# First pages and squares re-dealt, and the compressed decode branch laid out in rows, in a hybrid-decoder step on one core

## The chip, the cores and the metric

One core of a Trainium2 chip runs the kernel. The metric is device time in microseconds of one execution, the median of three. A measurement of this kernel can tell some 0.2% (2.3 us) from no change.

## The reference

One layer of a decoder step for 256 prompt tokens and 8 decode requests with 2048 past tokens each. RMS-normed inputs (2048 wide) go through one wide projection `w_in` in fp32. Two token mixers follow: sparse attention in three branches (compressed, selected, window) and a gated DeltaNet. Their outputs are gated, projected (`w_pa`, `w_pb`), merged, projected once more (`w_o`) and added to the input. The part that the change touches is the compressed branch of the decode requests:

```python
def nsa_sample(q, kv_cmp, kv_slc, kv_win, cache_cmp, cache_slc, st_win, page_table, cw, slopes):
    past = cache_cmp[page_table].reshape(DB, past_len, 2, NSA_KV_HEADS, HEAD_DIM)
    pk_past, pv_past = compress_partials(past, cw)      # conv over 16-token strides with w1
    kc, vc = compress_finish(...)                       # silu, w2, rms_norm of keys: 127 compressed K, V rows
    o_cmp, p_cmp = cmp_attend(q, kc, vc, qpos, slopes)  # softmax(q kc * SCALE - slope * distance) vc
    idx, valid = select_blocks(p_cmp, qpos, kc.shape[1], ...)   # top 16 blocks by summed p_cmp
    o_slc = slc_sample(...)                             # attention over the selected blocks, gathered from the cache
    o_win, _ = dense_gqa(...)                           # attention over the last 512 tokens
```

There are 8 requests, 2 key/value groups and 4 query heads per group: 64 softmax rows of 127 compressed keys. Each branch's output is scaled by a sigmoid gate per head; the three are added.

## The kernel before

The program is one long loop over "halves" (lines 1623 to 1636). A half is a block of 1024 rows of weights (512 KB) times the normed input, or a quarter of one request's pages of the compressed cache times `w1`: 24 matmuls of 254 or 264 columns, since each fp32 operand is split into `hi` (ScalarE, ACT) and `lo` (VectorE, DVE), both fp32r, and three of the four products are made. Turn i of the loop issues the load of half i+4, the split of half i+2 and the matmuls of half i; `hi` and `lo` have three buffers each.

Between a half's two parts, and behind it, stands `tick()`. Everything else (the input norm, the finishing of compressed keys, decode branches, prompt attention, DeltaNet) is a generator that a tick takes on to its next `yield`; `yield n` skips to the n-th tick from there. Ticks begin at turn -1: turn i makes ticks 2i+3 and 2i+4. Turns 0, 2, 4 and 6 load `w1` and have no matmuls; turns 1, 3, 5, 7 and from 8 on are page halves, four to a request; after the 24th come the projections of `kvc`, the first that need the normed input. Four parts of x, of four 128-row blocks each, are marked as they are ready; the program runs ticks ahead of a projection until the part that it needs is marked.

DMA queues of SP and POOL (GpSimd) keep the program's order. On PE (TensorE), ACT and DVE the framework that builds the kernel takes, among the instructions that are ready by its estimate, the one that the program issued first; the order is then fixed.

Big tiles share one pool of 13 slots (`slot()`, tag `s8`): cache pages, the input, `q`, keys, gates, DeltaNet tiles, gathered keys and values (`gk`, `gv`), probabilities (`sP`, `wP`) and the branch outputs `X`. A tile holds its slot until its last access.

Start: `load_pages` issues request 0's 16 pages of 128 KB over SP, POOL and ACT in turn (line 384), each after a `value_load` of its page number. `g_xnorm` (line 279) loads the parameters (`prm`), later constants (`cst`), then the input (`xt`), squares it on ACT, reduces over blocks on DVE (line 295), sums over partitions on PE (`xss`), takes a reciprocal root in 12 DVE steps (`rsq`, line 212), scales `xt` (line 306) and splits it into `xh`, `xl`.

The decode branches run one after the other (`g_dec_cmp`, `g_dec_slc`, `g_dec_win`, then `g_oa`). `g_dec_cmp` puts the 127 keys on partitions: for each group and request it multiplies that request's keys (128 columns of weights) with all 64 queries (`dcs`) and keeps the 4 columns that belong (`diag`); likewise the values (`dcv`). The result, scaled by `gd`, goes to `oD`. The other two branches use a row layout: 128 softmax rows, 32 for each of four column groups of PE, of which 16 are in use; products there have 32 columns of weights (`qk`, `gsc`, `wsc`, `pvo`). Their outputs `X0` and `X1` are turned into columns by `smo`, one product for each request and branch, and added to `oD`. `g_gdn` (DeltaNet of the prompt) and the `z` projections wait for what `g_oa` copies from `oD`.

Of the kernel before, what the change touches and what calls it, by code (L numbers as in the profile page):

```python
# [55 lines left out]
def shape_constants():  # L56
# [19 lines left out]
    sl64 = np.broadcast_to(slope.reshape(2, 1, 4), (2, NB, 4)).reshape(64)  # L76
    c.add("cmpb", -(PAST - kendd)[:, None] * sl64[None])
# [67 lines left out]
def program(tc, A):  # L145
# [93 lines left out]
    gd = cp.tile([128, 64], F32, name="gd")  # L239
    grow = cp.tile([128, 2], F32, name="grow")  # L240
# [132 lines left out]
    rawc = {}  # L373

    def load_pages(kv, b, part):
# [7 lines left out]
        for j in range(4 * part, 4 * part + 4):  # L383
            e = (SP, G, S)[j % 3] if kv + b == 0 else (SP, G)[j % 2]
# [218 lines left out]
    def g_small(ps):  # L603
# [24 lines left out]
        mm(p2[:, 0:64], ones[0:24, :], x[:, 0:2].rearrange("p a b r -> p (a b r)"))  # L628
        S.activation(gd, p2[:, 0:64], AF.Copy)
        xp = tp.tile([24, 2, 2, 2, 32], F32, name="gxp", tag="a", bufs=NA)  # L630
        V.memset(xp, 0.0)
        for br in range(2):
            for c in range(2):
                V.tensor_copy(xp[:, br, c, :, 0:16].rearrange("p g (i r) -> p g i r", r=4),
                              x[:, 2 + 2 * br:4 + 2 * br].rearrange("p a (i c) r -> p c a i r", c=2)[:, c])
            mm(p2[:, 192 + br:193 + br], xp[:, br].rearrange("p c g x -> p (c g x)"), ones[0:24, 0:1])
        V.tensor_copy(grow, p2[:, 192:194])
# [3 lines left out]
    def diag(ps, dst, g):
        d = dst[:, 32 * g:32 * g + 32].rearrange("p (b r) -> p b r", r=4)
        return [(d[:, 0:7], ps[:, 0:476].rearrange("p (b c) -> p b c", c=68)[:, :, 32 * g:32 * g + 4], slice(0, 7)),
                (d[:, 7:8], ps[:, 476 + 32 * g:480 + 32 * g].unsqueeze(1), slice(7, 8))]


    def g_dec_cmp():
# [3 lines left out]
        SCm = tp.tile([128, 64], F32, name="dcs", tag="dcs")  # L651
        E = tp.tile([64, 128], F32, name="dce", tag="zz", bufs=2)
        PT = tp.tile([128, 64], F32, name="dcp", tag="dcp")
        m1 = tp.tile([64, 4], F32, name="dcm", tag="dcm")
        qf = qd.rearrange("p g b r -> p (g b r)")
# [9 lines left out]
        p2 = psb("dct")
        tr(p2[0:64, 0:127], SCm[0:127, :])
        V.tensor_reduce(m1[:, 0:1], p2[0:64, 0:127], AX.X, ALU.max, negate=True)
        S.activation(E[:, 0:127], p2[0:64, 0:127], AF.Exp, bias=m1[:, 0:1], accum_out=m1[:, 1:2])
        V.reciprocal(m1[:, 2:3], m1[:, 1:2])
        V.tensor_scalar(E[:, 0:127], E[:, 0:127], m1[:, 2:3], None, ALU.mult)  # L670
# [15 lines left out]
        mark("oD")  # L686
# [78 lines left out]
    def row_softmax(sc, n, w):  # L765
# [8 lines left out]
        V.tensor_mul(sn[:, 3:4], sn[:, 3:4], grow[:, w:w + 1])  # L774
# [33 lines left out]
    def pv_take(po, w, b):  # L808
        if b % 4 == 3:
            S.activation(L["X", w][:, b - 3:b + 1, :], po.rearrange("p (b d) -> p b d", b=4), AF.Copy)  # L810

    def g_dec_win():
# [40 lines left out]
        sc = bb[:, 1]  # L853
        yield 7
# [24 lines left out]
        del L["X", 0], L["X", 1]  # L879
        mark("oD")  # L880

    def g_dec_slc():
# [13 lines left out]
        GP, VP = 1, 1  # L896
# [37 lines left out]
        L["X", 0] = slot("X0", [128, NB, 128])  # L934
        yield 2
        for b in range(NB):
# [6 lines left out]
            pv_take(po, 0, b)  # L943
# [798 lines left out]
```

## Time and profile before

| | |
|---|---|
| time, three runs | 1136.26, 1136.46, 1137.62 us (median 1136.46) |
| profiled execution | 1137.88 us, its span 1136.2 us |
| PE busy | 1112.4 us (98%) |
| DVE, ACT, POOL busy | 697.1, 572.7, 144.2 us |
| DMA | 222.17 MB, mean 196 GB/s |
| mean granted clock of PE | 0.994 |

The span runs from the first to the last instruction; the metric is a little longer. Engines: PE is TensorE's matmul, PEld its weight load. A product of plain fp32 appears as two instructions. Times in the rows below are us from the span's start.

### The profile page before, as it was taken

To read this page: it belongs to the slowest core of one execution; us is meant where nothing else is said; L and a number is where in the kernel's file an instruction comes from. 1 tells how busy PE (TensorE), PEld (TensorE's weight loads), DVE (VectorE), ACT (ScalarE), POOL (GpSimd) and SP (SyncE) were. 2 spreads that over 40 slices of the span, in tenths; PEclk is the share of its full clock that TensorE was granted. 3 is DMA by queue.
4 is the path that set the end of the run, shared out by engine and by line. 5 is a ranking of instruction groups with operands and counts; after the bars stand their busy time and mean duration, and the time that the engine had idled before them with its cause. 6 is when DMAs were issued, how large, how long until landed. Compare 5 with 4: busy or idle time off the path is not lost.

```text
span 1136.2 us, 25323 instructions
## 1 busy us (share of the span) xinstructions
PE 1112.4 (98%) x9558; PEld 1069.3 (94%) x9558; DVE 697.1 (61%) x1523; ACT 572.7 (50%) x1138; POOL 144.2 (13%) x227
## 2 busy tenths in 40 slices
PE   4999999999999999999999999999999999999998
PEld 3989999999999987897989999999999999999998
DVE  3578565443657776783566577677547575487443
ACT  4445655444634766673454465545344554444332
POOL 4430244200001310113022100102000000000000
PEclk9989999999999999999999899999999999999999
DMA  9873676435445784568998755657454355556663
GB/s 302 255 241 124 202 205 203 152 95 160 161 138 177 218 214 135 159 196 220 281 390 291 268 174 176 201 179 220 138 187 148 119 165 177 181 184 223 201 236 125
DMA packets 77069, 222.17 MB, mean 196 GB/s; under 512 B 10625, under 2 KB 27850, under 8 KB 75410
## 3 DMA queue, kind: packets, MB, share of 16 engines
q1 hardware_dynamic: 59346, 164.36, 44.7%
q0 software_dynamic: 15008, 44.98, 13.8%
q10 hardware_dynamic: 2592, 11.21, 2.6%
q8 instruction: 75, 1.23, 0.4%
q14 instruction: 48, 0.39, 0.1%
HBM read 202.90 MB, written 17.60 MB: 194 GB/s over the span
## 4 chain that ended last, share of the span: by engine, by line
PE 92%; DVE 1%; ACT 0%; issue 0%; ACTq 0%
PE acc L205 77%; PE inv L205 1%; PE po L205 1%; PE gtr L202 1%; PE pvo L205 1%; PE ps L205 1%; PE gsc L205 1%; PE cf L205 1%; PE kk L205 1%; PE vnb L202 1%; PE uw L205 1%; DVE xt L306 1%; PE pst L202 0%; PE og L205 0%; PE wsc L205 0%; PE kvtr L202 0%
## 5 line engine op out<-in xcount | busy, mean ns | idle before, releaser
L333 DVE TENSOR_TENSOR lo<-raw,hi 128x1024 fp32r<-128x1024 f32 (+1 forms) x250 | 304.8, 1220 | 212.5 <-ACT hi L332 206.1
L205 PE MATMUL acc<-xh,hi 128*128 128x264 f32 (+1 forms) x1488 | 433.8, 292 | 0.0
L332 ACT ACTIVATE hi<-raw 128x1024 fp32r<-128x1024 f32 (+1 forms) x250 | 263.9, 1056 | 329.7 <-PE acc L205 269.0
L205 PE MATMUL acc<-xl,hi 128*128 128x264 f32 (+1 forms) x1488 | 426.9, 287 | 0.5 <-issue 0.5
L205 PE MATMUL acc<-xh,lo 128*128 128x264 f32 (+1 forms) x1488 | 426.3, 287 | 0.0
L205 PEld LDWEIGHTS acc<-xh,hi 128*128 128x128 f32 (+1 forms) x1488 | 281.0, 189 | 7.6 <-issue 7.0
L205 PEld LDWEIGHTS acc<-xh,lo 128*128 128x128 f32 (+1 forms) x1488 | 280.0, 188 | 2.7 <-issue 2.2
L205 PEld LDWEIGHTS acc<-xl,hi 128*128 128x128 f32 (+1 forms) x1488 | 281.1, 189 | 1.5 <-issue 1.0
L205 PE MATMUL acc<-hi,w1h 128*128 128x254 f32 (+1 forms) x512 | 148.1, 290 | 15.9 <-ACT hi L409 15.9
L205 PE MATMUL acc<-lo,w1h 128*128 128x254 f32 (+1 forms) x512 | 147.4, 288 | 3.4 <-DVE lo L410 3.2
L205 PE MATMUL acc<-hi,w1l 128*128 128x254 f32 (+1 forms) x512 | 145.7, 285 | 0.0
L410 DVE TENSOR_TENSOR lo<-rawc,hi 128x512 fp32r<-128x512 f32 (+2 forms) x136 | 84.0, 656 | 52.5 <-ACT hi L409 48.1
L205 PEld LDWEIGHTS acc<-hi,w1h 128*128 128x128 f32 x512 | 98.4, 192 | 16.0 <-ACT hi L409 15.9
L409 ACT ACTIVATE hi<-rawc 128x512 fp32r<-128x512 f32 (+2 forms) x136 | 74.7, 599 | 62.7 <-PE acc L205 58.0
L205 PEld LDWEIGHTS acc<-lo,w1h 128*128 128x128 f32 x512 | 99.2, 194 | 4.8 <-DVE lo L410 4.5
L205 PEld LDWEIGHTS acc<-hi,w1l 128*128 128x128 f32 x512 | 99.0, 193 | 0.1
L386 POOL DMA_DIRECT2D rawc<-ccmp x125 | 67.3, 538 | 98.2 <-issue 72.3
L205 PE MATMUL acc<-oh,hi 128*128 128x264 f32 x256 | 73.5, 287 | 0.0
L205 PE MATMUL acc<-oh,lo 128*128 128x264 f32 x256 | 72.9, 285 | 0.0
L205 PE MATMUL acc<-ol,hi 128*128 128x264 f32 x256 | 72.7, 284 | 0.0
L205 PE MATMUL acc<-mh,hi 128*128 128x264 f32 x256 | 72.6, 284 | 0.0
L205 PE MATMUL acc<-ml,hi 128*128 128x264 f32 x256 | 72.5, 283 | 0.0
(452 smaller groups left out, 1476.4 us busy)
## 6 DMA issues: line engine op xcount, KB each, us to landing
raw<-win SPq DMA_DIRECT2D x184, 512.0 KB, 3.5
raw<-wpab SPq DMA_DIRECT2D x32, 512.0 KB, 3.9
raw<-wo SPq DMA_DIRECT2D x32, 512.0 KB, 4.3
rawc<-ccmp SPq DMA_DIRECT2D x126, 128.0 KB, 2.7
rawc<-ccmp POOLq DMA_DIRECT2D x125, 128.0 KB, 3.3
raw<-w SPq DMA_DIRECT2D x8, 512.0 KB, 7.6
wk<-winK SPq DMA_DIRECT2D x8, 512.0 KB, 11.1
o_wk<-wk POOLq DMA_DIRECT2D x8, 512.0 KB, 9.0
```

The source lines that it names most:

```text
L202: T.transpose(out, in_, ident[0:n, 0:n])
L205: T.matmul(out, lhsT, rhs, start=start, stop=stop, **k)
L306: V.scalar_tensor_tensor(xt[i][:, k, :], xt[i][:, k, :], P("nw")[:, kk:kk + 1], rx, ALU.mult, ALU.mult)
L332: S.activation(self.hi, self.raw, AF.Copy)
L333: V.tensor_sub(self.lo, self.raw, self.hi)
L386: e.dma_start(rawc[kv, b][j // 8][:, j % 8].rearrange("p s c g -> p (s c g)"), src[kv, bass.ds(r, 1)].rearrange("o d f -> (o d) f"))
L409: S.activation(h, src, AF.Copy)
L410: V.tensor_sub(l, src, h)
```

## The change

1. Request 0's pages are dealt by a list `FIRST`: 7 to SP, 6 to ACT, 3 to POOL (6, 5, 5 before). `prm` is issued three ticks later, `cst` and `xt` one tick later.
2. The squares of x are made in halves of four blocks with a tick between; the reduction over 8 blocks becomes three adds of 4, 2 and 1 blocks. In ticks the sum over partitions moves from 43 to 50.
3. `g_dec_cmp` uses the row layout: scores by `qk` with 32-column weights, key norms spread over rows by a transpose and a product, softmax over 128 rows, values by 32 products of 64 (63) rows and 32 columns of weights, outputs into one `X`.
4. The other branches add into the same `X` (DVE, from PSUM) instead of having their own; `smo` has 8 products for `X` instead of 16. The gates of all three branches come in row form (`grow`, three columns; `gd` goes).
5. In `g_dec_win` the second value load is issued before the scores, the others one step earlier; in `g_dec_slc` value gathers run two requests ahead instead of one.

```diff
-    c.add("cmpb", -(PAST - kendd)[:, None] * sl64[None])
+    c.add("kd", np.broadcast_to(-(PAST - kendd)[None], (128, NCMP)))
...
     def g_xnorm():
+        yield 3
         G.dma_start(prm, A["prm"])
+        yield 5
         V.tensor_scalar(hb[:, 0:1], P("b1k"), 0.5, None, ALU.mult)
         V.tensor_scalar(hb[:, 1:2], P("b1v"), 0.5, None, ALU.mult)
-        yield 7
         G.dma_start(cst, A["cst"])
...
         for i in range(2):
-            S.activation(sq, xt[i], AF.Square)
-            V.tensor_reduce(a2[i], sq.rearrange("p k t -> p t k"), AX.X, ALU.add)
+            for k in range(2):
+                S.activation(sq[:, 4 * k:4 * k + 4], xt[i][:, 4 * k:4 * k + 4], AF.Square)
+                yield
+            V.tensor_add(sq[:, 0:4], sq[:, 0:4], sq[:, 4:8])
+            yield
+            V.tensor_add(sq[:, 0:2], sq[:, 0:2], sq[:, 2:4])
+            V.tensor_add(a2[i], sq[:, 0], sq[:, 1])
+            yield
         V.tensor_add(a2[0], a2[0], a2[1])
-        yield 5
+        yield 3
...
+    FIRST = (SP, S, G, SP, S, SP, S, G, SP, S, G, SP, S, SP, S, SP)
...
-            e = (SP, G, S)[j % 3] if kv + b == 0 else (SP, G)[j % 2]
+            e = FIRST[j] if kv + b == 0 else (SP, G)[j % 2]
...
     def g_dec_cmp():
...
-        for g in range(2):
-            pt = psb("dcs")
-            for b in range(NB):
-                mm(pt[0:127, 64 * b:64 * b + 64], L["kcT"][:, b, g, :], qf)
-            for o, pv, w in diag(pt[0:127], SCm[0:127], g):
...
-        V.tensor_add(SCm[0:127], SCm[0:127], C("cmpb", 127))
+        tr(p2[0:16, 0:127], rkc[0:127])
+        rkt = tp.tile([16, 128], F32, name="rkt", tag="imp")
+        V.tensor_copy(rkt[:, 0:127], p2[0:16, 0:127])
+        mm(p2[:, 128:255], C("e64", 16), rkt[:, 0:127])
+        S.activation(rkr, p2[:, 128:255], AF.Copy)
+        pt = psb("dcs")
+        for i in range(4):
+            qk(pt, i, lambda c, g: L["kcT"][:, 2 * i + c, g, :])
+        V.tensor_mul(SC, pt[:, 0:127], rkr)
+        V.scalar_tensor_tensor(SC, C("kd"), C("c64")[:, 1:2], SC, ALU.mult, ALU.add)
...
         yield 5
...
+        tr(p3[0:127, 0:128], SC)
...
+        V.tensor_scalar(SC, SC, grow[:, 0:1], None, ALU.mult)
         yield 3
-        for g in range(2):
-            p5 = psb("dcv")
-            for b in range(NB):
-                mm(p5[:, 64 * b:64 * b + 64], L["vc"][0:127, b, g, :], PT[0:127, :])
-            for (o, pv, _), (_, gv, _) in zip(diag(p5, oD, g), diag(p5, oD, g)):
-                V.tensor_copy(o, pv)
-        V.tensor_mul(oD, oD, gd)
+        tr(p3[0:127, 128:256], SC)
+        S.activation(PT[0:127], p3[0:127, 128:256], AF.Copy)
...
+        yield 2
+        L["X"] = slot("X", [128, NB, 128])
+        for b in range(NB):
+            if b % 4 == 0:
+                po = PV("pvo")
+            for g in range(2):
+                for t, rows in enumerate((slice(0, 64), slice(64, 127))):
+                    j, c, o = 2 * g + t, 2 * (b % 2) + g, 128 * (b % 4)
+                    mm(po[32 * j:32 * j + 32, o:o + 128], PT[rows, 32 * c:32 * c + 32], L["vc"][rows, b, g, :])
+            if b % 4 == 3:
+                S.activation(L["X"][:, b - 3:b + 1, :], po.rearrange("p (b d) -> p b d", b=4), AF.Copy)
...
-    def pv_take(po, w, b):
+    def pv_take(po, b):
         if b % 4 == 3:
-            S.activation(L["X", w][:, b - 3:b + 1, :], po.rearrange("p (b d) -> p b d", b=4), AF.Copy)
+            x = L["X"][:, b - 3:b + 1, :]
+            V.tensor_add(x, x, po.rearrange("p (b d) -> p b d", b=4))
...
+        load_v(1)
         yield 7
         scores([ps], sc, bb[:, 0])
...
-            if b % 2 == 0 and b < 6:
-                load_v(b // 2 + 1)
+            if b % 2 == 0 and b < 4:
+                load_v(b // 2 + 2)
...
-        for w in range(2):
-            for b in range(NB):
-                mm(o[:, :, b, :], L["X", w][:, b, :], gx[:, :, b, :], start=False, stop=w * b == 7)
-        V.tensor_add(oD, oD, pt[:, 0:64])
+        for b in range(NB):
+            mm(o[:, :, b, :], L["X"][:, b, :], gx[:, :, b, :], start=False, stop=b == 7)
+        V.tensor_copy(oD, pt[:, 0:64])
...
-        GP, VP = 1, 1
+        GP, VP = 1, 2
```

## Rows read from the trace of the kernel before

**Rows 1.** The page: the span, and PE's busy time with its share and instructions.

```profile
span 1136.2 us, 25323 instructions
...
PE 1112.4 (98%) x9558; PEld 1069.3 (94%) x9558; DVE 697.1 (61%) x1523; ACT 572.7 (50%) x1138; POOL 144.2 (13%) x227
```

**Rows 2.** PE's waits of the whole span: who waited for whom, then us in total, times, longest.

```profile
PE acc L205 <- ACT hi L409: 15.9, 1, 15.9
...
PE acc L205 <- DVE lo L410: 3.2, 2, 2.6
...
PE pvo L205 <- ACT wP L798: 0.6, 1, 0.6
```

**Rows 3.** Stretches of the first 100 us: from:to, length, then busy us and instructions of PE, PEld, DVE, ACT and POOL, granted clock of PE, share of the DMA engines, GB/s.

```profile
40.00:50.00 10.00, 10.00 (x85) 9.95 (x85) 5.37 (x10) 5.62 (x12) 4.07 (x9) 1.00 0.72 224
...
71.00:72.00 1.00, 0.00 (x0) 0.00 (x0) 1.00 (x3) 0.27 (x1) 0.36 (x1) 0.98 0.34 131
...
77.00:78.80 1.80, 1.80 (x9) 1.59 (x8) 0.43 (x1) 0.02 (x1) 0.08 (x1) 0.50 1.00 292
...
78.80:80.00 1.20, 1.20 (x11) 1.20 (x12) 1.09 (x4) 1.14 (x2) 0.55 (x1) 1.00 0.99 364
...
90.00:100.00 10.00, 9.90 (x83) 9.51 (x82) 10.00 (x19) 7.91 (x11) 0.00 (x0) 1.00 0.10 21
```

**Rows 4.** The same table for two stretches after 635 us.

```profile
635.10:638.00 2.90, 2.90 (x15) 2.90 (x16) 0.17 (x1) 1.06 (x1) 0.00 (x0) 0.51 1.01 406
...
642.00:644.00 2.00, 2.00 (x18) 2.00 (x18) 0.00 (x0) 0.00 (x0) 0.00 (x0) 1.00 0.22 76
```

**Rows 5.** PE's timeline from 630 us: start, us, instruction, its operands, count (a row's length reaches to the end of its last instruction, which overlaps the next row).

```profile
630.90 1.46 PE L205 MATMUL smo<-cst,X 128*128 128x8 f32 x12
...
632.47 2.30 PE L205 MATMUL smo<-cst,X 128*128 128x8 f32 x20
...
634.62 1.36 PE L205 MATMUL dec<-smt,cst 128*128 128x8 f32 x8
```

**Rows 6.** DVE's timeline between 60 and 73 us, in the same form.

```profile
60.95 4.22 DVE L295 TENSOR_REDUCE xa<-xsq 128x264 f32<-128x2112 f32 x1
...
67.20 4.14 DVE L295 TENSOR_REDUCE xa<-xsq 128x264 f32<-128x2112 f32 x1 [0.85 <-ACT xsq L294]
...
71.27 1.26 DVE L410 TENSOR_TENSOR lo<-rawc,hi 128x512 fp32r<-128x512 f32 x2
```

**Rows 7.** Timelines of PE and of DVE between 77 and 102 us: the sum of squares, a finishing step of the compressed keys, the first product with `xl`; then DVE's first step on the sum of squares and its last `xl`.

```profile
77.24 1.08 PE L205 MATMUL xss<-xa,cst 128*128 128x264 f32 x2
...
90.78 0.50 PE L205 MATMUL cf<-cst,csq 128*127 128x1 f32 x4
...
98.12 0.37 PE L205 MATMUL acc<-xl,hi 128*128 128x264 f32 x1
...
78.36 0.43 DVE L217 TENSOR_SCALAR rqx<-xss 128x264 f32<-128x264 f32 x1 [2.74 <-PE xss L205]
...
101.53 1.27 DVE L311 TENSOR_TENSOR xl<-xt,xh 128x1056 fp32r<-128x1056 f32 x1
```

**Rows 8.** The start: the stretch from 10 to 15 us in the table's form, the issue of request 0's pages on ACT's and SP's queues, and the `hi` that releases PE.

```profile
10.00:15.00 5.00, 0.00 (x0) 0.00 (x0) 2.26 (x4) 1.67 (x3) 3.20 (x6) 1.00 0.99 319
...
3.08 4.92 ACTq L386 DMA_DIRECT2D rawc<-ccmp  x5
...
15.19 1.67 ACT L409 ACTIVATE hi<-rawc 128x512 fp32r<-128x512 f32 x3 [3.35 <-DMA rawc<-ccmp]
...
3.17 6.02 SPq L386 DMA_DIRECT2D rawc<-ccmp  x6
```

**Rows 9.** PE's timeline of the compressed decode branch: scores, and what follows them; values, and what follows them.

```profile
315.21 1.88 PE L205 MATMUL dcs<-qd,kcT 128*127 128x64 f32 x16
...
316.90 0.36 PE L205 MATMUL acc<-xh,lo 128*128 128x264 f32 x1
...
334.53 3.68 PE L205 MATMUL dcv<-dcp,vc 127*128 127x64 f32 x32
...
338.02 0.37 PE L205 MATMUL acc<-xl,hi 128*128 128x264 f32 x1
```

**Rows 10.** PE's timeline of the selected branch's value products, and what follows the first 26.

```profile
512.21 1.06 PE L205 MATMUL pvo<-gv,sP 120*32 120x128 f32 x26
...
513.21 0.55 PE L202 MATMUL pst<-cst,zz 128*128 128x128 f32 x3
```

**Rows 11.** Instructions by tile (line, engine, operation and tile, count: shortest, median and longest ns, first and last start in us; shapes), and one of POOL's waits.

```profile
L205 PE MATMUL gsc<-gkx,qm x64: 566/566/590, 402.1 to 488.0; 128*32 128x480 f32 x64
...
L924 DVE TENSOR_TENSOR sb<-sbias,cst x1: 2041/2041/2041, 482.1 to 482.1; 128x960 f32<-128x960 f32 x1
...
L798 ACT ACTIVATE sP<-ptr x2: 581/585/589, 505.8 to 506.3; 120x512 f32<-120x512 f32 x2
...
L205 PE MATMUL po<-PTt,kTa x24: 592/592/697, 446.6 to 526.9; 128*128 128x512 f32 x24
...
L1583 DVE COPY qT<-oD x2: 179/182/186, 639.2 to 639.3; 128x32 f32<-128x32 f32 x2
...
L1491 DVE SCALAR_TENSOR_TENSOR zt<-zt,qT x8: 426/433/434, 645.8 to 756.7; 128x264 f32<-128x264 f32 x8
...
POOL gv L891 <- PE ptr L202: 14.2, 1, 14.2
```

More of the change, by code (lines that the diff above doesn't have):

```diff
@@ L238, in program @@
     smt = cp.tile([128, 2, 72], F32, name="smt")
-    gd = cp.tile([128, 64], F32, name="gd")
-    grow = cp.tile([128, 2], F32, name="grow")
+    grow = cp.tile([128, 3], F32, name="grow")
     acc2 = cp.tile([128, 128], F32, name="acc2")
@@ L627, in g_small @@
         p2 = psb("gdp")
[L628 to L632, printed above, removed]
+        for br in range(3):
+            xp = tp.tile([24, 2, 2, 32], F32, name="gxp", tag="a", bufs=NA)
+            V.memset(xp, 0.0)
             for c in range(2):
[L634 to L637, printed above, removed]
+                V.tensor_copy(xp[:, c, :, 0:16].rearrange("p g (i r) -> p g i r", r=4),
+                              x[:, 2 * br:2 * br + 2].rearrange("p a (i c) r -> p c a i r", c=2)[:, c])
+            mm(p2[:, br:br + 1], xp.rearrange("p c g x -> p (c g x)"), ones[0:24, 0:1])
+        V.tensor_copy(grow, p2[:, 0:3])
         V.tensor_scalar(beh, smt[:, :, 64:72], 0.5, None, ALU.mult)
         mark("small")
[L641 to L644, printed above, removed]
     def g_dec_cmp():
@@ L650, in g_dec_cmp @@
         yield from wait("cd", 16)
[L651 to L655, printed above, removed]
-        for g in range(2):
-            pt = psb("dcs")
-            for b in range(NB):
-                mm(pt[0:127, 64 * b:64 * b + 64], L["kcT"][:, b, g, :], qf)
-            for o, pv, w in diag(pt[0:127], SCm[0:127], g):
-                V.tensor_tensor(o, pv, rkc[0:127, 8 * g + w.start:8 * g + w.stop, None].to_broadcast([127, w.stop - w.start, 4]),
-                                ALU.mult)
@@ L663, in g_dec_cmp @@
-        V.tensor_add(SCm[0:127], SCm[0:127], C("cmpb", 127))
-        yield 5
[L665 to L670, printed above, removed]
+        SC = tp.tile([128, 127], F32, name="dcs", tag="a", bufs=NA)
@@ new lines, in g_dec_cmp @@
+        PT = tp.tile([128, 128], F32, name="dcp", tag="a", bufs=NA)
+        m1 = tp.tile([128, 4], F32, name="dcm", tag="dcm")
+        p2 = psb("dct")
+        tr(p2[0:16, 0:127], rkc[0:127])
+        rkt = tp.tile([16, 128], F32, name="rkt", tag="imp")
+        V.tensor_copy(rkt[:, 0:127], p2[0:16, 0:127])
+        mm(p2[:, 128:255], C("e64", 16), rkt[:, 0:127])
+        rkr = tp.tile([128, 127], F32, name="rkr", tag="a", bufs=NA)
+        S.activation(rkr, p2[:, 128:255], AF.Copy)
+        pt = psb("dcs")
@@ L671, in g_dec_cmp @@
+        for i in range(4):
+            qk(pt, i, lambda c, g: L["kcT"][:, 2 * i + c, g, :])
+        V.tensor_mul(SC, pt[:, 0:127], rkr)
+        V.scalar_tensor_tensor(SC, C("kd"), C("c64")[:, 1:2], SC, ALU.mult, ALU.add)
+        V.tensor_reduce(m1[:, 0:1], SC, AX.X, ALU.max, negate=True)
+        S.activation(SC, SC, AF.Exp, bias=m1[:, 0:1], accum_out=m1[:, 1:2])
+        V.reciprocal(m1[:, 2:3], m1[:, 1:2])
+        V.tensor_scalar(SC, SC, m1[:, 2:3], None, ALU.mult)
+        yield 5
         p3 = psb("dct")
-        tr(p3[0:127, 0:64], E[:, 0:127])
@@ L683, in g_dec_cmp @@
-        V.tensor_mul(oD, oD, gd)
+        for c in range(2):
+            V.tensor_reduce(PR[0:127].rearrange("p (g i c) -> p c g i", g=2, c=2)[:, c],
+                            p3[0:127, 64 * c:64 * c + 64].rearrange("p (g x) -> p g x", g=2)[:, :, 0:16]
+                            .rearrange("p g (i r) -> p g i r", r=4), AX.X, ALU.add)
+        V.tensor_scalar(SC, SC, grow[:, 0:1], None, ALU.mult)
+        yield 3
+        tr(p3[0:127, 128:256], SC)
+        S.activation(PT[0:127], p3[0:127, 128:256], AF.Copy)
@@ L773, in row_softmax @@
         V.reciprocal(sn[:, 3:4], sn[:, 3:4])
-        V.tensor_mul(sn[:, 3:4], sn[:, 3:4], grow[:, w:w + 1])
+        V.tensor_mul(sn[:, 3:4], sn[:, 3:4], grow[:, w + 1:w + 2])
         V.tensor_mul(sn[:, 4:5], sn[:, 4:5], sn[:, 3:4])
@@ L859, in g_dec_win @@
         P_ = pt_rows("wP", sc, 4, 128)
-        L["X", 1] = slot("X1", [128, NB, 128])
         for b in range(NB):
-            if b % 2 == 0 and b < 6:
-                load_v(b // 2 + 1)
+            if b % 2 == 0 and b < 4:
+                load_v(b // 2 + 2)
             if b % 4 == 0:
@@ L868, in g_dec_win @@
             pv_part(po, P_, 128, b, range(4), 4, lambda g, t: vr[b // 2][:, b % 2, t, 128 * g:128 * g + 128])
-            pv_take(po, 1, b)
+            pv_take(po, b)
         yield 5
@@ L874, in g_dec_win @@
         mm(pt[:, 0:64], acc2, C("perm"), start=True, stop=False)
[L875 to L879 removed]
+        for b in range(NB):
+            mm(o[:, :, b, :], L["X"][:, b, :], gx[:, :, b, :], start=False, stop=b == 7)
+        V.tensor_copy(oD, pt[:, 0:64])
+        del L["X"]
         mark("oD")
@@ L933, in g_dec_slc @@
         P_ = pt_rows("sP", sc, 8, 120)
-        L["X", 0] = slot("X0", [128, NB, 128])
         yield 2
@@ L942, in g_dec_slc @@
             pv_part(po, P_, 120, b, range(8), 8, lambda g, t: vr[b][0:120, g, t, :])
-            pv_take(po, 0, b)
+            pv_take(po, b)
             vr[b] = None
@@ L1580, in g_oa @@
         yield from wait("attn")
-        yield from wait("oD", 2)
+        yield from wait("oD")
         for g in range(2):
```

4 lines of the change are left out of this document (removed).

## The prediction

> **What bounds the kernel now.** I read the page first. TensorE (PE) is busy 1112.4 of 1136.2 us and its chain is the path [rows 1]; every other engine has slack. So time can only come from two places: PE instructions that go away, and stretches in which PE stands or runs slow. The list of PE's waits names nearly all the standing: 15.9 us before the first matmul and 3.2 us on the low halves of the page products, of which 2.6 at once [rows 2]. The stretches with their granted clock show the running slow. About 70 us PE does next to nothing (71 to 72: no matmul at all), and from 72 the clock is 0.50, the lower level, until 78.8 [rows 3]. The same happens after 635.1, until 642 [rows 4]. Each stretch of half clock is 6.8 to 6.9 us and so costs half of that, 3.4 us. What came before them differs: before the first PE stood; before the second it was busy without a break, but with 8-column matmuls, from 630.9 to 635 [rows 5].
>
> **Squares of x.** The wait at 70 us is made by VectorE (DVE): two reductions over `xsq` of 4.2 and 4.1 us, at 60.95 and 67.20, and the page products' `lo` at 71.27 behind the second; PE's matmul waits for it [rows 6]. The change replaces each reduction by three adds over 1056, 528 and 264 elements. The trace has one of 1056 elements, 1.27 us [rows 7]; scaled, that is 1.27 + 0.64 + 0.32, an estimate of 2.2 us in place of 4.2, and no piece over 1.3. A `lo` then waits 1.3 us at most, and PE's operands are made two halves ahead, so I cost the wait of 2.6 and the slow clock behind it at nothing: 2.6 + 3.4 = 6.0 us won at 79 us.
>
> Most of it I expect to be lost again 20 us later. The sum of squares (`xss`) goes from tick 43 (1+7+30+5) to tick 50 (1+3+5+30, eight for the pieces, 3). Tick 50 is the end of turn 23, after 20 page halves. The four small `cf` matmuls at 90.78 are where the program puts them, after 22 halves; a half is 24 matmuls of 0.118 us [rows 3], 2.82 us; so 20 halves end at 90.78 - 5.6 = 85.1, and without the 6.0 lost at 79.1 [rows 7]. `xss` today starts at 77.24, at the slow clock, and DVE takes it up at 78.36. So it does not come earlier; DVE gets it at some 79.6. From there to the end of the last `xl`, 78.36 to 101.53 + 1.27 = 102.8, DVE has 24.4 us of work with hardly a break (from 90 to 100 it is busy 10.00 of 10.00 [rows 3, 7]). What is in it stays (12 steps of rsqrt, 16 scalings, 4 `xl`), but PE is 6 us, two halves, further on, so two halves' `lo` (1.26 a half [rows 6]) are already made: 21.9 us, to 101.5. PE asks for the first `xl` at 98.12 today, at 92.1 then, and for each further one after 12 matmuls, 1.4 us. So it stands in pieces behind DVE until 101.5, and is then where it is today at 102.8: 1.3 us kept of 6.0. Ends: all 6.0 if `xss` gets in earlier or PE finds other work, and -2.1 if the clock falls in these waits (1.3 less 3.4). I take 1.3, since the rows show DVE full there.
>
> **First pages.** Sixteen pages are dealt anew: SP 7, ScalarE (ACT) 6, POOL 3 in place of 6, 5, 5. PE's start hangs on the last page: the second set of `hi` at 15.19 waits for it [rows 8]. From 10 to 15 us the DMA engines are at 0.99 [rows 8], so the bytes decide, and they are the same (`cst` grows by 63 columns of 128x4 bytes, 32 KB). ACT and SP issue one more page, 1.0 us each [rows 8], and POOL's parameters and constants go out two pages earlier, beside the last pages. I take 0, ends -1.1 and +1.1. Nothing else rests on the following: the Trainium skill (Trainium Kernel Development and Optimization, Key Constraints) says that the three issuing queues share the same 16 engines and that more issuers save only issue time; the share of 0.99 agrees, and it speaks against any gain here.
>
> **Compressed decode branch.** This is PE work on the path. It removes:
> - 16 score products, 32 instructions `dcs`: two groups of 16, the first from 315.21 to 316.90, 1.69 us each: 3.38 [rows 9].
> - 16 value products, 32 `dcv`: 334.53 to 338.02: 3.49 [rows 9].
> - 8 of the 16 products that gather the branches' outputs (`smo`): 32 instructions now, of which 20 take from 632.47 to 634.62, 2.15 us [rows 5], 0.108 each; 16 go: 1.73.
>
> It adds 16 score products with 32 columns of weights (32 instructions, like `gsc`) and 32 value products likewise (64). The nearest rows are `pvo`: 26 in the 1.00 us from 512.21 to 513.21, 0.038 each [rows 10]. 96 x 0.038 = 3.65. A transpose of `rkc` and its spreading are three more at most at 0.11: 0.35. The gates' row form has six tiny instructions where six were; two transposes stay two. Sum: 8.6 - 4.0 = 4.6 us less. Bounds: the value products use half the rows at a time, which no row shows with 32 columns; at the pace of `dcv`, 0.109, they would cost 7.0 in place of 2.4 and the gain be nothing; at half of it, 1.2, and the gain 5.8. I take `pvo`: same columns, same way of placing outputs.
>
> By themselves stand these sentences: the Trainium skill (TensorE: Matmul & The Clock Gate, Part 3: Packing small matmuls) gives three column tiles a measured 2.38 times. From the full-weight 0.109 an estimate by that is 0.046 each, 4.4 us for the 96, and a sum 0.8 us smaller; the `pvo` rows, at 0.038, are better than it.
>
> DVE and ACT do about as much as before here (softmax in 128 rows instead of 64; four adds into `X` on DVE where ACT copied). It is hidden behind PE, which was busy all through; uncovered, what waits is the weights' `lo`, queued behind on DVE.
>
> **The second slow stretch.** The 8-column work before 635.1 is 2 + 32 `smo` and 8 `dec`, with two transposes between: at 0.108 each 4.5 us. With 16 fewer it is 2.8. The row in evidence for a shorter stretch is the `dcv` group: 3.49 us of narrow matmuls (64 columns), and no fall. I take the stretch as gone, 3.4 us won; the other end is 0.
>
> **Loads and slots.** `load_v(1)` goes before the scores, and value gathers run two ahead. PE waits for neither; its one later wait for data is 0.6 us on `wP` [rows 2]: 0. `X` holds one of 13 slots from the compressed branch on, where today the first is taken after the selected branch's softmax. While that branch transposes its keys, the code holds twelve (`qT`, `qm`, `kTa`, a gate, `qkvr`, `ktk`, two each of `PTt`, `gk`, `gkx`); `X` is the thirteenth. I take 0; a rival below prices the rest.
>
> **Sum.** 1.3 + 0 + 4.6 + 3.4 = 9.3 us. The profiled execution took 1137.88, so 1128.6; the median of the runs shown is 1.42 below it: 1136.46 - 9.3 = 1127.2.
>
> **Rivals.**
> - The 6.0 us at 70 are kept, because `xss` is put earlier or PE fills its waits. For: DVE has free time from 72 on. Against: its fullness after 78. 1136.46 - 14.0 = 1122.5.
> - The slow clock stays at 635, or moves to another place (the waits for `xl`): for, the stretch before it is still narrow. 1127.2 + 3.4 = 1130.6; with both 1134.0.
> - Slower: the slots run out. At 482 `qkvr` and `sb` both want one, while `gkx` is read to 488.0; at 505 `sP` must follow `sb`, and POOL's second gather ahead, no longer held by a step of the program, asks for the same slot (today a gather waits 14.2 us for `sb`'s transposes) [rows 11]. If the gather wins, `sP` waits for `PTt`, read to 526.9: 21 us later than 505.8. The branch's sum reaches `oA` at 639.3 and is read at 645.8 [rows 11]: 6.5 us of cover. 21 - 6.5 = 14.5 us of PE waiting, 1127.2 + 14.5 = 1141.7. It decides from a delay of 6.5 + 9.3 = 15.8 us.
> - The row layout saves nothing: the half-row products run at 0.109 and the narrow stretch stays: 9.3 - 4.6 - 3.4 = 1.3, 1135.2, within what can be told from no change.
>
> **How the numbers follow.** Chances: forecast 0.47, the 6.0 kept 0.14, slow clock stays or moves 0.19, slots 0.13, nothing saved 0.07. Predicted is the first, 1127.2; its own range is 1124.5 to 1130, from the bounds of the pages (1.1) and of the products (1.2 better) and half of the loss by a fall of the clock. The range for 8 in 10 takes in the second and third cases and leaves out the slots and nothing saved: 1122 to 1134. A measurement here tells 0.2%, 2.3 us, from no change: faster 0.80, same 0.07, slower 0.13.
>
> **What would show it.** Squares: no wait of PE at 70 us and full clock from 21 to past 90; then PE waits named `xl` or `xt` at 92 to 101, together 4 to 5 us. Products: 32 + 64 narrow instructions at 0.038 in place of 64 at 0.108. Gather: 16 `smo` fewer and a clock of 1.00 all through 630 to 645. Slots: `sP` within 3 us of the last transpose of `sb`. It is wrong if DVE's x chain no longer sets PE about 100, if the half clock shows anywhere new, or if PE waits between 480 and 650.

## The result, and the profile after

The changed kernel takes 1146.95 us (median of four, 1146.65 to 1150.47) against 1136.36 us for the kernel before on the same chip: ratio 1.0101, interval 1.0086 to 1.0117. It is slower by 10.6 us where 9.3 us of gain was forecast. The page, and after it the first seven of PE's waits (us in total, times, longest), which answer to [rows 1, 2]:

```profile
span 1145.0 us, 25339 instructions
...
PE 1108.8 (97%) x9577; PEld 1065.5 (93%) x9577; DVE 696.8 (61%) x1529; ACT 573.8 (50%) x1139; POOL 146.4 (13%) x225
```

```profile
PE acc L204 <- ACT hi L415: 18.8, 2, 18.4
PE acc L204 <- DVE xl L316: 3.3, 1, 3.3
PE pvo L204 <- DMA gv<-cslv,idx: 2.5, 1, 2.5
PE rrow L201 <- DVE aT L1188: 1.5, 1, 1.5
PE acc L204 <- DVE lo L338: 1.3, 1, 1.3
PE cf L204 <- ACT csq L462: 1.2, 1, 1.2
PE kk L204 <- DVE edl L1174: 1.0, 1, 1.0
```

PE is busy 3.6 us less, and idle 36.2 us instead of 23.8. The wait of 2.6 us on `lo` is gone; six new ones of 1.0 to 3.3 us stand in four places (95 to 99, 553, 650 and 706 to 708 us). The stretches (from:to, length, busy us and instructions of PE, PEld, DVE, ACT, POOL, granted clock, DMA share, GB/s) show half clock behind three of them, and at 637 us behind the 8-column products, as in [rows 3, 4]:

```profile
94.00:98.00 4.00, 0.99 (x5) 0.70 (x5) 4.00 (x9) 3.46 (x8) 0.00 (x0) 0.99 0.30 81
98.00:104.70 6.70, 5.54 (x25) 5.54 (x26) 6.15 (x7) 1.06 (x1) 0.00 (x0) 0.50 0.32 112
...
552.00:555.30 3.30, 1.98 (x38) 1.79 (x39) 0.78 (x4) 0.00 (x0) 0.00 (x0) 1.00 1.03 269
555.40:558.70 3.30, 3.30 (x17) 3.30 (x17) 0.47 (x1) 1.53 (x3) 0.00 (x0) 0.50 1.01 287
637.30:640.60 3.30, 3.30 (x17) 3.10 (x16) 1.94 (x6) 1.75 (x2) 0.00 (x0) 0.50 1.05 254
709.00:715.70 6.70, 6.16 (x28) 6.16 (x29) 2.31 (x8) 2.57 (x7) 0.00 (x0) 0.50 0.09 39
```

Where the time went is read by setting the n-th weight or page matmul of one trace against the n-th of the other, 24 to a half: the time in the changed kernel less the time before. This curve stands at +2.5 us at the first, +1.4 after 6 halves (37 us), -4.5 after 24 (93 us), +3.7 after 27 (111 us), +4.3 until 312 us, -3.0 at 488 us, +2.7 after 147 (562 us), -1.4 after 180 (687 us), +9.7 after 186 (718 us), +6.8 after 190 (730 us), +8.5 from 925 us to the end. So the loss has four places: the start, 93 to 111 us, 545 to 562 us, and 687 to 718 us. Two cautions go with the curve. It is drawn against one execution of the kernel before (1137.88 us), which is slower than that kernel's medians (1135.3 to 1137.1). And it also moves when another step is shifted past the weight products and nothing is lost: f1 below, which costs nothing, stands at -10.5 after 125 halves. What was lost is counted by PE's idle time and the half clock. Between 600 and 760 us, the kernel before and then the changed one:

```profile
600.00:760.00 160.00, 160.00 (x1411) 156.91 (x1410) 103.49 (x234) 81.38 (x160) 15.82 (x24) 0.98 0.64 218
600.00:760.00 160.00, 154.97 (x1363) 149.59 (x1363) 102.77 (x226) 80.21 (x156) 14.60 (x22) 0.97 0.61 208
```

PE is idle 5.0 us there where it was idle 0.0, and the half clock at 709 costs half of the 6.16 us in which PE is busy in it: some 8 us in all, where the curve rises by 11.1 between 687 and 718 us and falls again by 2.9 behind.

**The start** [rows 8]: SP's page issues, POOL's constants, and the `hi` that releases PE, now at 17.72; then the stretch from 10 us, and the constants in the list of DMA issues.

```profile
3.14 7.14 SPq L392 DMA_DIRECT2D rawc<-ccmp  x7
...
9.51 0.53 POOL L283 DMA_DIRECT2D cst<-cst  x1
...
17.72 1.67 ACT L415 ACTIVATE hi<-rawc 128x512 fp32r<-128x512 f32 x3 [4.88 <-DMA rawc<-ccmp]
```

```profile
10.00:15.00 5.00, 0.00 (x0) 0.00 (x0) 2.42 (x5) 1.99 (x5) 2.73 (x6) 1.00 0.94 337
```

```profile
cst<-cst POOLq DMA_DIRECT2D x1, 911.0 KB, 7.9
```

**The x chain** on DVE [rows 6, 7]: adds instead of reductions, the first step on the sum of squares, the last three `xl`.

```profile
62.35 1.25 DVE L296 TENSOR_TENSOR xsq<-xsq 128x1056 f32<-128x1056 f32 x1
...
64.72 0.70 DVE L298 TENSOR_TENSOR xsq<-xsq 128x528 f32<-128x528 f32 x1
65.46 0.43 DVE L299 TENSOR_TENSOR xa<-xsq 128x264 f32<-128x264 f32 x1
...
81.14 0.43 DVE L216 TENSOR_SCALAR rqx<-xss 128x264 f32<-128x264 f32 x1 [1.29 <-PE xss L204]
...
100.57 3.58 DVE L316 TENSOR_TENSOR xl<-xt,xh 128x1056 fp32r<-128x1056 f32 x3
```

**The compressed branch** on PE [rows 9], and the first value gather behind `sP` on POOL [rows 11]; last the gather of the same request in the kernel before:

```profile
323.40 1.07 PE L204 MATMUL dcs<-kcT,qm 128*32 128x127 f32 x32
...
340.60 1.08 PE L204 MATMUL pvo<-vc,dcp 64*32 64x128 f32 x32
...
508.53 1.11 POOL L898 DMA_INDIRECT gv<-cslv,idx  x1 [32.80 <-ACT sP L805]
```

```profile
489.49 0.96 POOL L891 DMA_INDIRECT gv<-cslv,idx  x1 [11.52 <-ACT cth L1082]
```

That gather is request 1's. It went out at 489.49; now it comes 19 us later.

**700 to 710 us**, PE without its weight products: two DeltaNet steps in a row, both waiting for DVE, and no weight product between them. Below them two of the steps in the kernel before: 8.4 us apart, with 60 weight products between.

```profile
703.75 1.16 PE L204 MATMUL kk<-qkvr 128*128 128x128 f32 x8
706.44 0.40 PE L201 MATMUL rrow<-cst,dec 128*128 128x128 f32 x2 [1.53 <-DVE aT L1188]
707.81 1.13 PE L204 MATMUL kk<-qkvr 128*128 128x128 f32 x8 [0.97 <-DVE edl L1174]
```

```profile
696.33 1.05 PE L205 MATMUL kk<-qkvr 128*128 128x128 f32 x8
703.02 0.38 PE L202 MATMUL rrow<-cst,dec 128*128 128x128 f32 x2
704.70 1.05 PE L205 MATMUL kk<-qkvr 128*128 128x128 f32 x8
```

### The profile page after: what moved, and what is told of

Same layout as the page of the kernel before. It is cut to its first block, busy times and chain, and to the rows that moved or that the text cites. A ratio compares the mean times of both kernels' runs of the same rounds, so it can differ in the third digit from the quotient of the medians.

```text
span 1145.0 us, 25339 instructions
## 1 busy us (share of the span) xinstructions
PE 1108.8 (97%) x9577; PEld 1065.5 (93%) x9577; DVE 696.8 (61%) x1529; ACT 573.8 (50%) x1139; POOL 146.4 (13%) x225
## 4 chain that ended last, share of the span: by engine, by line
PE 66%; DMA 3%; ACT 1%; DVE 1%; issue 0%; POOL 0%; SPq 0%; ACTq 0%
PE acc L204 53%; DMA gv<-cslv,idx 1%; PE inv L204 1%; PE po L204 1%; PE gtr L201 1%; DMA wv<-winV 1%; PE ps L204 1%; PE pvo L204 1%; PE gsc L204 1%; PE vnb L201 1%; PE uw L204 1%; PE og L204 0%; PE kk L204 0%; PE pst L201 0%; PE wsc L204 0%
```

## The experiments

All ratios are to the kernel before on the same chip, with 95% intervals. "X late" (below) means that the compressed branch's output goes through `smo` at once and X takes its slot only behind the selected branch's softmax; "two ticks out" removes the `yield 2` ahead of the value products; "sum early" cuts the ticks ahead of x's loads so that the sum of squares stands at tick 43 again (42 in e8, e12 and f4, where the old order of `prm` takes a tick less).

| kernel | us | ratio | order 640 to 720 |
|---|---|---|---|
| changed kernel | 1146.95 | 1.0101 [1.0086, 1.0117] | bunched |
| first pages alone (e1) | 1138.1 | 1.0014 [1.0002, 1.0026] | spread |
| squares alone (e2) | 1138.8 | 1.0020 [1.0009, 1.0031] | spread |
| decode alone (e3) | 1142.1 | 1.0042 [1.0030, 1.0054] | bunched |
| changed, sum early (e4) | 1141.4 | 1.0044 [1.0029, 1.0060] | bunched |
| e4, two ticks out (e5) | 1149.7 | 1.0115 [1.0098, 1.0133] | bunched |
| e5, one gather ahead (e6) | 1151.2 | 1.0135 [1.0099, 1.0170] | bunched |
| e5, X late (e7) | 1133.8 | 0.9983 [0.9968, 0.9997] | spread |
| e6, old pages (e8) | 1147.3 | 1.0106 [1.0079, 1.0132] | bunched |
| changed, X late (e9) | 1149.9 | 1.0127 [1.0108, 1.0146] | bunched |
| e4, X late (e10) | 1141.9 | 1.0066 [1.0047, 1.0085] | bunched |
| e7, one gather ahead (e11) | 1135.1 | 0.9996 [0.9981, 1.0011] | spread |
| e7, old pages (e12) | 1133.0 | 0.9974 [0.9957, 0.9991] | spread |
| before, two ticks (f1) | 1135.4 | 0.9998 [0.9988, 1.0007] | spread |
| before, X0's slot held (f2) | 1142.2 | 1.0057 [1.0045, 1.0069] | spread |
| e3, ticks out, X late (f3) | 1149.0 | 1.0118 [1.0095, 1.0141] | bunched |
| e12, old window loads (f4) | 1142.3 | 1.0058 [1.0045, 1.0071] | bunched |
| before, squares, sum early (f5) | 1131.6 | 0.9968 [0.9957, 0.9979] | spread |
| changed, DeltaNet loop 2 ticks back (f6) | 1146.7 | 1.0095 [1.0081, 1.0110] | bunched |

"Bunched" is read from the trace: a PE wait for `hi` or `lo` of weights at 640 to 653 us and waits of DeltaNet's `rrow` or `kk` for DVE at 700 to 719; "spread" has neither.

**One part alone (e1 to e3), and the sum early (e4).**

```
e1  FIRST and the yields around prm alone      e2  squares and adds alone
e3  - FIRST, prm order, squares                e4  - yield 30    + yield 23
```

> The kernel before with the first pages of the changed kernel alone (dealing, and parameters and constants three turns later). Theory A, the start's loss stays: in the changed kernel the first matmul comes at 18.40 us instead of 15.87 and 1.4 us of it are still there at 37 us, so 1136.4 + 1.4 to 2.5 = 1137.8 to 1138.9. Rival, the loss is taken up again where TensorE waits for VectorE at 70 us anyway: 1136.4, no change. A full change at 15.19 -> 18.40 in the first matmul is expected by both.

> The kernel before with the squares and sums of x in pieces alone; the sum of squares still moves from tick 43 to tick 49. Theory A, the late tick: the stall at 70 us and its 3.4 us of half clock go (-5.7 by the changed kernel), and TensorE stands for xl and at half clock at 93 to 105 us (+8.2 there): 1136.4 + 2.5 = 1138.9. Rival, the step as predicted: 1.3 us kept, 1135.1. Rival, all is kept since the pages are not late: 1130.7.

> The changed kernel with the first pages and the squares of the kernel before: row layout, one X, value gathers two ahead and the early value load alone. Theory A, the losses at 553 us (2.5 us wait for a gather, 1.7 for half clock) and at 700 to 716 us belong to this part: after 110 us the changed kernel loses 8.5 - 4.3 = 4.2 us, so 1136.4 + 4.2 = 1140.6. Theory B, they belong to the phase that the first 110 us set (tick work falls differently), and this part has the 4.6 us of narrow products that were costed: 1131.8. Half clock near 553 and 709 shows A, full clock there shows B.

> The changed kernel with the 30 ticks before the loads of x cut to 23, so that the sum of squares stands at tick 43 again as before. Theory A, the tick of the sum is what made TensorE stand at 93 to 105: the wait of 3.3 us for xl and the half clock of 6.8 us there go and the 8.2 us lost in that stretch come back, 1147.0 - 8.2 = 1138.8. Rival, VectorE's load is what counts and not the tick: the wait moves a few us earlier, 1147.0 within 1. Rival, downstream phase: after 110 us the same shift makes the stretches at 553 and 709 us differ by +-4 us.

e1 (`prm` three ticks later, `cst` and x one tick): the loss of the start stays (1.6 us, 0.2 to 3.0). e2: the late tick costs more than the squares bring, as theory A had it. e4 gives some 6 us back (+4.3 us against before, where the changed kernel has +10.6) and its x stretch is clean; but 700 to 716 stays as it was. e3 says that the decode part, without the others, loses 4.8 us, the most of the three parts (theory A); by the ratios the three alone make 1.6 + 2.3 + 4.8 = 8.7 us and together 11.5, which is no difference beyond the intervals. In e3's trace the curve against before falls from -2.3 at 306 us to -7.9 after 138 halves (502 us), and all of it is lost again later. That fall is not the worth of the row products alone: f1, which has the same two ticks and the old products, falls by 1.8 over the same halves, which leaves 3.8.

**The squares without the delay (f5)**, against e2: stretches of e2, then of f5, then f5's DVE rows.

```
f5  kernel before + squares in pieces;  - yield 30   + yield 24
```

> The kernel before with the squares in pieces, and the 30 ticks cut to 24, so that the sum of squares stays at tick 43; no page and no decode change. Theory G, the late sum is all that was wrong with the squares: no wait of 2.6 us at 72 us, no half clock there, no wait for xl at 99, so all of the 6.0 us are kept: 1135.9 - 5 to 6 = 1130.4. Rival, the step as it was put on record, VectorE's x chain binds to 101.5 whatever the tick: 1.3 kept, 1134.6. Rival: what is won is lost where the DMA engines are full (505 to 560 us): 1133 to 1136.

```profile
94.00:98.00 4.00, 1.43 (x8) 0.84 (x6) 4.00 (x9) 4.00 (x7) 0.00 (x0) 1.00 0.06 17
98.50:105.00 6.50, 5.63 (x25) 5.63 (x26) 5.86 (x7) 0.82 (x1) 0.00 (x0) 0.50 0.47 161
```

```profile
72.00:80.00 8.00, 8.00 (x68) 7.95 (x68) 7.20 (x18) 3.40 (x8) 3.11 (x6) 1.00 0.93 311
...
94.00:98.00 4.00, 4.00 (x35) 4.00 (x34) 3.38 (x4) 2.12 (x3) 0.00 (x0) 1.00 0.88 272
98.50:105.00 6.50, 6.50 (x56) 6.50 (x55) 2.55 (x3) 3.14 (x5) 0.00 (x0) 1.00 0.67 246
```

```profile
68.86 0.42 DVE L217 TENSOR_SCALAR rqx<-xss 128x264 f32<-128x264 f32 x1
...
92.48 1.25 DVE L317 TENSOR_TENSOR xl<-xt,xh 128x1056 fp32r<-128x1056 f32 x1
```

The last `xl` ends at 93.7 and PE's only wait there is 0.5 us for a `hi`. The curve is -6.0 at the end: theory G holds in the trace. The medians show 3.7 us, and they decide: the one execution in which the kernel before was profiled has a granted clock of 0.994, and 16 of the 17 on this chip have 0.995 or 0.997, so most of them had less half clock to win back. This kernel is faster than both.

**The slot (f2), the ticks (f1), and both undone in the changed kernel (e5 to e12).**

```
f1  mm(p4[0:16, 0:30], ...)                f2  mm(p4[0:16, 0:30], ...)
    + yield 2                                  + L["X", 0] = slot("X0", ...), one column set
                                               - the same line behind sP
e7  + smo of X, V.tensor_copy(oD, ...), del L["X"] at the end of the compressed branch
    + L["X"] = slot("X", ...) behind sP;  V.tensor_add(oD, oD, ...) at the last smo
```

> The kernel before with two ticks more in the compressed branch and nothing else. Theory E, the ticks alone make the loss at 700 to 716 us: every run with these two ticks shows the same three waits there (1.53 us for aT, 0.97 for edl, 0.6 for a gate) and loses 8 to 9 us; then 1136 + 7 = 1143. Rival, ticks and slot only together, or the row layout, make it: no such waits, 1136 within 1.5.

> The kernel before with X0's slot taken in the compressed branch and held (one column of it is set there), the row layout left out. Theory F, the slot alone delays the second value gather from 489 us to behind sb's transposes at some 505, and gathers bunch: waits for gv at 545 to 555 us of 2 to 5 us with half clock after, and DeltaNet's decode states late: 1136 + 7 to 12 = 1143 to 1148. Rival: a loss only where TensorE has become faster ahead of the gathers: 1136 to 1139.

f1: nothing, theory E falls. f2: the gather is late, as theory F has it, and holding one slot, with no other change, costs 6.4 us (1142.2 against 1135.8), a little less than its 7 to 12. The place is another than it named: PE waits for no `gv`, DeltaNet loses nothing, and the loss lies at 530 to 541 us. POOL's request 1 waits for `sb`'s transposes; below it stand PE's value products, then two stretches of f2, and last the same stretches of the kernel before (clock and DMA share are the third and second columns from the end):

```profile
504.27 1.27 POOL L893 DMA_INDIRECT gv<-cslv,idx  x1 [28.08 <-PE ptr L202]
...
531.05 0.27 PE L205 MATMUL pvo<-gv,sP 120*32 120x128 f32 x1 [0.30 <-issue]
531.77 0.41 PE L205 MATMUL pvo<-gv,sP 120*32 120x128 f32 x4 [0.45 <-issue]
533.20 0.42 PE L205 MATMUL pvo<-gv,sP 120*32 120x128 f32 x3 [1.02 <-issue]
534.61 1.01 PE L205 MATMUL pvo<-gv,sP 120*32 120x128 f32 x10 [1.00 <-issue]
```

```profile
530.00:536.00 6.00, 2.92 (x25) 1.64 (x24) 2.81 (x6) 1.85 (x3) 2.66 (x4) 0.82 1.02 246
536.00:540.60 4.60, 4.60 (x23) 4.60 (x23) 1.13 (x1) 1.36 (x2) 1.85 (x2) 0.50 1.05 232
```

```profile
530.00:536.00 6.00, 5.49 (x68) 4.98 (x66) 3.51 (x8) 3.23 (x7) 3.63 (x5) 1.00 0.96 234
536.00:540.60 4.60, 4.60 (x63) 4.24 (x62) 1.67 (x5) 2.04 (x4) 0.41 (x1) 1.00 1.04 239
```

The late gathers bunch, the DMA engines are full, PE does its products in drops, and half clock follows. That the full engines make the drops was not shown: at 536.00 in the kernel before they stand at 1.04, from 525 to 530 us in e7 at 1.05, and PE is busy throughout. The same drops stand in e3 and e4 (2.2 and 2.6 us of "issue"); the changed kernel waits for `gv` instead.

> The changed kernel with the sum of squares early (30 ticks cut to 23) and without the yield of 2 ticks ahead of the value products: with both, each later stage stands at the same tick beside the same halves as in the kernel before. Theory C: between 685 and 716 us the early-sum kernel loses 7.5 + 2.0 = 9 us of which 2 are given back, and again 2 to 3 us at 860 to 890, because DeltaNet's prompt part starts two ticks later and its steps meet other work. Then the half clock at 703 us goes and the time is 1141.4 - 8 = 1133.4, faster than before (1137). Rival: the loss comes from the slots or from VectorE's load, whatever the tick: 1141.4 within 1.5.

> As the previous one, with value gathers one request ahead again (VP 1). Theory D: two ahead makes six gathers fall together at 519 to 527 us, the DMA engines stand at 1.0, and 32 pvo products that take 1.08 us elsewhere take 6.1 us, with half clock after (528 to 535 us): with one ahead 5 us of drip and 3.4 us of clock come back, about 8 us less than the kernel of the previous run (1133.4 -> 1125). Rival: the gathers are held by slots and not by the number asked for, so they bunch just the same: no change, within 1 us. Rival: the DMA engines are the bound from 505 to 560 and the wait only moves to a gather: 0 to -3.

> As the run before the last one (two gathers ahead), but the compressed branch's output is turned into columns at once (8 products smo more, 0.9 us) and X gets its slot only behind the selected branch's softmax, as X0 had it before: no slot is held from 345 to 500 us. Slot theory: the second value gather goes out at some 489 us again in place of 501.9, and the bunch at 519 to 527 us and the half clock behind it go: 8 - 0.9 = 7 us less than the run with ticks alone (1133.4 -> 1126). Rival (two ahead is the cause, not the slot): 0.9 more, 1134.3.

> As the run with one gather ahead, with the dealing of request 0's pages and the place of parameters and constants undone. The first matmul comes back from 17.9 us to 14.4 to 15.9, and the time falls by 1.0 to 1.7 us against that run, by the run of the first pages alone. Rival: the start's gain is lost again behind the first pages of the next request (waits at 27 us): no change.

> The changed kernel with one edit alone: the compressed branch's output goes through smo at once (8 products more, 0.9 us), and X takes its slot only behind the selected branch's softmax. Slot theory: the second value gather no longer waits for sb's transposes (out at some 15 us before sP's end instead of 508.5), no wait for gv at 553, no half clock at 555, and the stretch at 700 to 716, which follows from late window loads and late states, loses nothing: from 110 us on the curve falls by 5.3 us as in the run of X late with the ticks back, and not rise by 4.2: 1147.0 - 9.5 = 1137.5. Rival: the repair needs the earlier sum or the two ticks too, 1147 + 0.9 = 1147.9.

> As the previous one, and the sum of squares at tick 43 again (30 ticks to 23), the two ticks of the compressed branch kept. Theory: both gains add, since they lie in stretches of their own (93 to 105 us, and from 500 us on): 1137.5 - 5.6 = 1131.9, against 1133.8 measured with the two ticks taken out. Rival: the two ticks cost 8 us as first thought: 1142. Rival: ticks decide by chance which work meets which, and with the slot free it no longer matters: 1133.8 within 2.

> X late, sum early and the two ticks out (1133.8), with value gathers one request ahead in place of two. If two ahead is worth something where slots are free, the last gathers come later and TensorE waits for gv: +1 to +4. If one ahead suffices, the DMA engines being full from 505 to 560 us either way: 1133.8 within 1.5.

> X late, sum early and the two ticks out (1133.8), with request 0's pages, the parameters and the constants as in the kernel before. The pages alone cost 1.0 to 1.7 us: 1132.4, the fastest of all. Rival: the start's 2 to 3 us (first matmul at 14.3 to 15.9 us in place of 17.8) are lost again at the next pages: 1133.8.

Most of these expectations missed. e5 is 8 us slower than e4 where 8 faster was expected, so theory C falls. e6: one gather ahead helps nothing (rival right). e7 is 16 us faster than e5 by X late alone, where some 7 were expected; in its trace, the fastest of its twelve executions, request 1 goes out at 481.84, PE waits 0.5 us for `gv`, and nothing is lost at 700. e8's first matmul comes back to 14.29 us, as expected, and its median is 4.0 us under e6's, within the intervals. Yet e9 and e10, X late with the ticks kept, gain nothing (for e10 a rival had said so), though request 1 goes out at 491.5 and 485.6. There requests 3 to 7 go out together, from 522.96 and 517.13 on, PE waits 2.0 and 2.9 us for `gv`, and half clock follows at 553.3 and 549.1: the slot of X is not the only thing that bunches gathers, and how much of the loss at 553 us in the changed kernel it makes is open. Nor has an edit a worth of its own here: taking the two ticks out costs 8 us where X is held (e4 to e5) and wins 8 where it is late (e10 to e7), and in the kernel before they cost nothing (f1). e11 and e12 differ from e7 by about a microsecond, within their intervals; repeats of e7 alone reach from 1128.55 to 1137.31 us.

**What is left open (f3, f4, f6).**

> The decode part alone (start and squares as before), with X late and the two ticks out. If the row layout has the worth that was costed, 4.6 us and up to 3.4 of half clock, less 0.9 for 8 products more: 1136 - 3.7 to 7.1 = 1129 to 1132. Rival: the gain is bounded by the full DMA engines at 505 to 560 and shows half: 1133 to 1135.

> The fastest so far (pages as before, sum early, ticks out, X late, 1133.0), with the window's value loads in their old place, one step later. If the 4.0 us wait for wv at 621 us, in the run before, comes from loads that are issued together with others, it goes: 1133.0 - 2 to 5 = 1129. Rival: loads one step later come later: the wait grows, 1134 to 1136.

> The changed kernel with one edit: in the DeltaNet part the 7 ticks ahead of its loop over heads are cut to 5, which puts that loop beside the same projections as in the kernel before. If the two ticks by which the loop moved make the loss between 640 and 720 us, its waits (lo at 650, aT, edl and gate at 706 to 710) and the half clock at 709 go: 1147 - 8 to 10 = 1138. If that order comes from what is ahead of it (the late gathers and loads), it stays: 1147 within 2.

f3 and f4 missed, and f6 stays at 1146.7, as its rival had it. In f4 the wait for `wv` falls from 4.0 to 2.1 us, as expected, and the time rises by 9.3. f3 is e12 with the old squares and the old tick count, its decode is the same and its gathers as early (484.3 against 484.1); it waits 5.7 us for `wv` at 622 (e12: 4.0) and is bunched. Two stretches of e12, then of f3:

```profile
640.00:660.00 20.00, 20.00 (x170) 19.86 (x173) 15.51 (x40) 8.99 (x15) 0.00 (x0) 1.00 0.54 158
700.00:710.00 10.00, 10.00 (x86) 10.00 (x84) 6.90 (x14) 5.32 (x10) 0.00 (x0) 1.00 0.45 152
```

```profile
640.00:660.00 20.00, 17.29 (x147) 16.72 (x150) 13.99 (x36) 8.49 (x14) 0.00 (x0) 0.91 0.41 135
700.00:710.00 10.00, 8.43 (x94) 7.78 (x93) 7.99 (x22) 5.61 (x14) 0.00 (x0) 1.00 0.43 153
```

So the runs fall into two groups, and every bunched kernel is 1141 us or more (so is f2, which is spread and loses at 530 us). The group follows from no single edit: not from the ticks (f1, f6), not from the slot (f2, e9), not from the place of window loads alone (f4 and f3 have different ones).

The traces show that the groups differ in the order of PE's instructions, and not only in their times. Between halves 170 and 200 the longest run of weight products with no other step in it is 168 in all eleven bunched kernels, and 83 or 84 in all nine spread ones. In e12 and f3 every other step stands beside the same dozen of weight products from half 27 (some 108 us) to half 170 (650 us) and again from half 191 on; between 170 and 190 it does not. The code of that stretch is the same in both; the edit that parts them is in the first 100 us. The order on PE, ACT and DVE is fixed when the kernel is built, by the framework's estimate: so in this pair a small shift far ahead turned it over. What in the estimate does it was not shown.

## Why the prediction was wrong, step by step

Forecast were 9.3 us won, and 10.6 were lost. The 19.9 between them, as far as the two traces count it: some 8 behind the decode branch, 3.6 in the x chain, 3.1 at the gathers, 2 at the start and 1.7 at the second slow stretch.

- **640 to 720 us**: in no step, and the largest single piece. The prediction let PE run everything behind the decode branch in the order of before, without saying so, and so put the cost of another order at nothing. The runs showed another order in its place: 5.0 us of PE's idle time and some 3 of half clock at 709. A rival had half clock moving elsewhere, but no DeltaNet step as its place.
- **Squares, the stall**: right. 5.9 us came back between 37 and 93 us (forecast 6.0); a reduction of 4.2 us became adds of 1.25 + 0.70 + 0.43 = 2.4 us (estimate 2.2).
- **Squares, the x chain**: the wait came much as forecast, 1.2 us on `csq` and 3.3 on `xl` where 4 to 5 on `xl` or `xt` were. The failed step is "I take 1.3", which left the fall of the clock in these waits to the low end (-2.1). PE did 0.99 us of work in 4.00 and then ran 6.8 us at half clock. The sum came at 81.14, not 79.6, and the last `xl` ended at 104.15, not 101.5; 1.4 us of both is the late start. 8.2 us were lost, so 2.3 net in place of 1.3 won. f5 shows that the tick, and not DVE's load, made the loss: with 43 the sum comes at 68.86 and the chain ends at 93.7.
- **First pages**: 0 forecast, 2.5 us late at the first matmul, 1.4 from 37 us on, 1.6 alone (e1). In all traces the first matmul comes at 14.0 to 16.3 us with the old pages and at 17.7 to 18.4 with the new. The step "the bytes decide, and they are the same" overlooked their order: POOL has two pages less, so `cst` (911 KB) now goes out at 9.51, ahead of SP's last page, which is issued at 9.94 and lands at 17.62; at 337 GB/s `cst` takes an estimated 2.8 us. That it is `cst` and not the dealing is argued, since no run parts the two.
- **Compressed branch**: right, and a little low. 32 score instructions take 1.07 us [rows 9], 32 half-row value instructions 1.01 from 340.60 to 341.61: 0.032 to 0.033 each against 0.038 taken, so 3.1 us for the 96 in place of 3.65. The 0.046 that the prediction estimated from the packing figure of the Trainium skill (TensorE: Matmul & The Clock Gate, Part 3) was too dear here.
- **Second slow stretch**: half right, 3.4 us of half clock at 637 instead of 6.8 at 635, so 1.7 won of 3.4. But the number of 8-column products does not decide it: with the same 16 `smo` fewer, e3 has 6.8 us (632.1 to 638.9) and e4 none, and f1, which has all the old ones, has 3.4 (at 638.5). What decides it was not shown.
- **Slots and loads at nothing**: wrong, and by the mechanism that a rival named. But the victim was not `sP` (507.3 against 505.8): the gather was late, bunched with the others, and the DMA engines were full. Alone this costs 6.4 us (f2), not the rival's 14.5; in the changed kernel the stretch from 480 to 600 us costs some 3 (PE idle 2.5 us, 1.1 before, and 1.7 of half clock).
- **The range**: its lower end by its own terms is 1127.2 - 1.1 - 1.2 = 1124.9, not 1124.5.

The tells held: the prediction was to be wrong if half clock showed anywhere new (97.95, 555, 709) or if PE waited between 480 and 650 (2.5 us at 553).

## What to carry to other kernels

Count a moved step in the units that the program is emitted in: seven ticks of 12 products (1.4 us) are 10 us, more than the 6 us that the change was to win. A tile held longer in a shared pool is a cost of its own, which falls on whoever allocates next, and an edit that leaves PE's work alone can still turn over an order that the build fixes, 500 us further on. Time the parts of a combined change one by one, since here one of them alone, with its tick kept, is faster than both kernels.

## What the runs showed of the hardware

With the DMA engines at 1.02 of their time, PE's narrow products, which run 32 in 1.08 us elsewhere, came in drops 0.7 to 1.4 us apart in f2 and the trace names no instruction that they waited for ("issue", 3.1 us); the half clock behind them lasted 6.8 us. A full share alone does not do it: in e7 32 of the same products take 1.08 us at 527.60, with the engines at 1.05. Value products of 64 rows and 32 columns of weights cost what those of 120 rows cost: 1.08 us for 32 at 340.60 in the changed kernel, and 1.08 for 32 at 531.24 in the kernel before.
